# Moving value differences into the convolution stage, splitting the queries and keys of two heads at once, and running the value products four blocks behind the transposes with five buffers

## The chip, the cores and the metric

The kernel runs on one core of one Trainium2 chip. The metric is device microseconds of one execution, from the program's start to its end; lower is better. The time before is the median of three runs, 2573.38 us.

The core has five engines that each work through their own queue in order: TensorE (PE in the profile; PEld is its weight load), VectorE (DVE), ScalarE (ACT), GpSimd (POOL) and SyncE (SP), which here issues all DMA transfers. TensorE writes to PSUM, which this kernel deals out in tiles of 128 partitions by 512 float32 values (called banks here); the other work memory is SBUF. Scratch tensors lie in DRAM.

## The reference, cut to what matters

One layer of a decoder trunk over 1024 tokens of width 1024: token mixing, cross-attention, feed-forward. The token mixing has three branches that start from one input projection; the change concerns the first, stick-breaking attention with 16 heads of 64:

```python
for blk in range(seq // SB_BLOCK):
    z = jnp.einsum('bhtd,bhsd->bhts', qf[:, :, t0:t1], kf[:, :, :t1])
    causal = jnp.arange(t1)[None, :] < (t0 + jnp.arange(SB_BLOCK))[:, None]
    log_1mb = jnp.where(causal, jax.nn.log_sigmoid(-z), 0.0)
    tail = lax.cumsum(log_1mb, axis=3, reverse=True)
    w = jnp.where(causal, jnp.exp(z + tail), 0.0)
    outs.append(jnp.einsum('bhts,bhsd->bhtd', w, vf[:, :, :t1]))
```

The weight of key s for query t is the difference of two neighbouring running products of sigmoid(-z). So the sum over keys of weight times value can be written as a sum over keys of (running product minus 1) times the difference of two neighbouring values. The kernel does that: it needs the running products, from one scan, and the value differences v[s-1] - v[s].

## The kernel before, in words

Matrix products are exact to nearly float32 by splitting each operand into a high part (fp32r) and a low part (the remainder): a copy on ACT or POOL makes the high part (`hi_sb`, L96 or L92), a subtraction makes the low part (`lo_of`, L99), and three products replace one (`mm3`, L102 to L104; `acc3`, L220 to L222).

The stages of the program, by the trace of before: input norm and the token-major projections, which write the values to the scratch tensor `v_d` (shifted by one row, so that v[s-1] and v[s] are two loads of the same tensor); the convolution stage, 293 to 641 us; the attention stage, 641 to 1090 us; then the state-space mixer, the output projections, cross-attention and the feed-forward.

**Convolution stage** (L634 to L729). It makes 36 blocks of 128 output channels, two at a time in `pair` (L681): 12 pairs of convolution channels and 6 pairs of gate channels, mixed in the list `order` so that a gate pair stands after one or two convolution pairs and one gate pair stands last. A pair loads weights of 1 MB (L193), POOL makes sums of them (L196 to L199), ACT and DVE split them, and `winograd_pair` (L224) does seven products of 12 matmuls each and adds them up in two tiles `y` of the pool `t4`, which has six buffers named "b4" (shown as `b`). The first copies out of PSUM into `y` are L230, L232 and L234, the last one L688. Then `conv` (L663) runs four taps on ACT and DVE into another buffer (L665 to L669), or `gate` (L677) takes the sigmoid (L678) and stores to `g_d` (L679). Transposes of a convolution pair (`tail`, L651) run after the products of the next pair.

**Attention stage** (L736 to L937). The work is a list of 32 items m, two per head: the first half of the queries (four blocks of 128) and the second. A head pair is four items. For each item three lists are merged by position:

- `values` of item m: step i transposes key block i of the running products (L868) into PSUM, ACT makes the high part of the weights (L871, `wth`), DVE the low part (L872, `wtl`), and the two value products of block i - LAG follow (L880, L881), with LAG = 3. A first half has 4 key blocks and 7 steps, a second half 8 key blocks and 11 steps.
- `scores` of item m + 1: for each of four query blocks, products of q with the high and low key parts (L849, L850) into the pool `psc`, the sigmoid on ACT (L851) and the running product on DVE as one scan (L852). They take positions 0 to 0.7 of the item.
- a quarter of the projections of q and k for a later head pair (`dense`, L758 to L778, 24 to 27 matmuls of 512 columns), or at the end of late gate blocks. Their results are taken out of PSUM by `ev_q` (L786) and `ev_k` (L797): for each of the two heads a copy on ACT makes the high part on 64 partitions (L794, L806) and a subtraction on DVE the low part (L795, L807). For q the low part goes to the upper 64 partitions; for k SP copies high and low part to the upper 64 partitions (L808, L809), so that one product covers two of the terms.

The first block of a head also calls `differences` (L822): for an even head SP loads two 512 KB tiles from `v_d` (L828) and POOL subtracts them (L829); for each head POOL makes high and low part (L92, L99).

In this stage eight banks of PSUM are dealt out as 2 for the projections, 3 for scores (`psc`), 2 for transposes (`pst`) and 1 for value products. The weights' pool `wt` has four buffers for each part.

The order on each engine isn't written out by hand: a planner goes through the program in order of priority with a model of time, so a blocked instruction can be overtaken by a later one of the program, and the order that comes out is fixed in the program. What is fixed by hand are the lists merged above and a mark that keeps projection matmuls from going too far ahead (`issue_behind`, L773).

Of the kernel before, what the change touches and what calls it, by code (L numbers as in the profile page):

```python
# [8 lines left out]
F32 = mybir.dt.float32  # L9
# [3 lines left out]
ALU = mybir.AluOpType  # L13
# [22 lines left out]
def hybrid_block(ctx, tc, a, out, dbg=None):  # L36
# [20 lines left out]
    def scr(name, shape, dt=F32):  # L57
        return dram.tile(shape, dt, tag=name, name=name)
# [6 lines left out]
    bt_d = [scr(f"bt_d{g}", [S, P]) for g in range(NG)]  # L65

    v_d = scr("v_d", [S + 1, D])
    g_d = scr("g_d", [2 * D, S])
    o_d = scr("o_d", [D, S])

# [16 lines left out]
    def hi_sb(o, i, eng=None):  # L87
        if eng is None:
            turn[0] += 1
            eng = "pa"[turn[0] % 2]  # L90
        if eng == "p":
            G.tensor_scalar(o, i, 1.0, 0.0, ALU.mult, ALU.add)  # L92
        elif eng == "v":
            V.tensor_copy(o, i)
        else:
            A.activation(o, i, AF.Copy)  # L96
# [154 lines left out]
    with ExitStack() as pa:  # L251
# [382 lines left out]
        with ExitStack() as p1:  # L634
# [43 lines left out]
                A.activation(y, y, AF.Sigmoid)  # L678
                nc.sync.dma_start(g_d[f * P:(f + 1) * P, :], y)  # L679
# [12 lines left out]
            jobs = [(C_X + f * P, f, conv) for f in list(range(16, 24, 2)) + list(range(0, 16, 2))]  # L692
            gts = [(C_GA + f * P, f, gate) for f in range(0, 16 - LATE_GATES, 2)]
# [42 lines left out]
        with ExitStack() as p2:  # L736
# [45 lines left out]
            def qk_proj(hp):  # L782
                for j in range(2):
                    heads[2 * hp + j] = {}

                def ev_q(ps, half):  # L786
                    sl = slice(half * HALF, (half + 1) * HALF)
                    for j in range(2):
# [3 lines left out]
                        pj = ps[j * HD:(j + 1) * HD]  # L792
                        q = hd["q"]
                        A.activation(q[0:HD, sl], pj, AF.Copy)  # L794
                        V.tensor_tensor(q[HD:P, sl], pj, q[0:HD, sl].bitcast(F32), ALU.subtract)  # L795

                def ev_k(ps, half):  # L797
                    sl = slice(half * HALF, (half + 1) * HALF)
                    for j in range(2):
# [4 lines left out]
                        pj = ps[j * HD:(j + 1) * HD]  # L804
                        kh, kl = hd["kh"], hd["kl"]
                        A.activation(kh[0:HD, sl], pj, AF.Copy)  # L806
                        V.tensor_tensor(kl[0:HD, sl], pj, kh[0:HD, sl].bitcast(F32), ALU.subtract)  # L807
                        nc.sync.dma_start(kh[HD:P, sl].bitcast(F32), kh[0:HD, sl].bitcast(F32))  # L808
                        nc.sync.dma_start(kl[HD:P, sl].bitcast(F32), kl[0:HD, sl].bitcast(F32))  # L809

                return dense(C_Q + hp * P, ev_q), dense(C_K + hp * P, ev_k)

# [7 lines left out]
            dvs = {}  # L820

            def differences(h):  # L822

                j = h % 2
                if j == 0:
                    va, vb = [mk(vp, [P, NCH, P], F32, n, bufs=1) for n in ("va", "vb")]
                    for t, r in ((va, 0), (vb, 1)):
                        nc.sync.dma_start(t, v_d[r:S + r, h * HD:(h + 2) * HD].rearrange("(c p) d -> p c d", p=P))  # L828
                    G.tensor_tensor(va, va, vb, ALU.subtract)  # L829
                    dvs[0] = va  # L830
                dv = dvs[0][:, :, j * HD:(j + 1) * HD]
                vt = mk(vp, [P, NCH, P], F32R, "v")
                hi_sb(vt[:, :, 0:HD], dv, "p")
                lo_of(vt[:, :, HD:P], dv, vt[:, :, 0:HD], G)
                heads[h]["v"] = vt

            def scores(h, half, tb, ns_):
                def run():
                    hd = heads[h]
                    if half == 0 and tb == 0:  # L840
                        differences(h)
                    b = half * 4 + tb
                    L = (b + 1) * P
                    nt = mk(bp, [P, (half + 1) * HALF], F32, f"n{half}")
                    ns_.append(nt)
                    for s0 in range(0, L, HALF):
                        s1 = min(L, s0 + HALF)
                        ps = mk(psc, [P, HALF], F32, "sc")[:, :s1 - s0]
                        T.matmul(ps, hd["q"][:, b * P:(b + 1) * P], hd["kh"][:, s0:s1], start=True, stop=False)  # L849
                        marks.append(T.matmul(ps, hd["q"][:, b * P:(b + 1) * P], hd["kl"][:, s0:s1], start=False, stop=True))  # L850
                        A.activation(nt[:, s0:s1], ps, AF.Sigmoid, scale=-(HD ** -0.5))  # L851
                    V.tensor_tensor_scan(nt[:, 0:L][:, ::-1], nt[:, 0:L][:, ::-1], mask[:, S - L:][:, ::-1], 1.0, ALU.mult, ALU.max)  # L852
                return run

            ots = {}

            LAG = 3

            def values(h, half, ns_):

# [1018 lines left out]
```

## Time and profile before

| | us |
|---|---|
| median of 3 runs | 2573.38 |
| lowest and highest run | 2568.3, 2574.95 |
| the profiled execution, whole | 2569.1 |
| its span, first to last instruction | 2567.4 |
| convolution stage, from the trace | 293 to 641 |
| attention stage, from the trace | 641 to 1090 |

The profile is of one execution. For each group of instructions it gives the busy time, the mean duration of one in ns, and the idle time of the engine just before them with what ended that idle time (the releaser). In the lists of waits each line has the waiting engine and line, what it waited for, the total in us, the number of waits and the longest. In the windows view the busy time of each engine in a stretch is given with the number of instructions, then TensorE's granted clock as a share of the full one, the share of time that the DMA engines were busy, and what they moved in GB/s. In the timeline a line has the start, the duration, the instruction and, in brackets, the idle time before it. A matmul is drawn longer than the distance to the next one, since matmuls overlap in the array.

### The profile page before, as it was taken

Reading aid. Unit: us, or ns where it says so; the run is one execution under the profiler, and the core shown is the slowest. Engines: PE = TensorE matmul, PEld = TensorE weight load, DVE = VectorE, ACT = ScalarE, POOL = GpSimd, SP = SyncE. Lnnn points to the kernel's source line nnn. Section 1 sums busy time; section 2 is a strip of 40 time slices with the busy share of each in tenths; the row PEclk is TensorE's granted clock in tenths of the full one; section 3 lists DMA queues with packets and bytes.
Section 4 is the critical chain, followed back from the end, with each engine's and each line's share of the span. In section 5 each row is a group of like instructions: output and inputs, shape, how many; then the busy total and the mean of one; then the engine's idle time right before and its main releaser. Section 6 shows DMA issues by size and latency. Waiting matters only on the chain.

```text
span 2567.4 us, 32619 instructions
## 1 busy us (share of the span) xinstructions
PE 2485.3 (97%) x12026; PEld 2059.4 (80%) x12026; DVE 1817.7 (71%) x2143; ACT 1149.7 (45%) x2052; POOL 824.6 (32%) x666
## 2 busy tenths in 40 slices
PE   8999999999999999989999999999999999999998
PEld 6788788887788788777888788888787888887776
DVE  7685777767689898678788654415459666666997
ACT  6343455655466666556544302314233333334433
POOL 4331533221211121135655231100114333333675
PEclk9999999999999999989999999999999999999999
DMA  6441433333322222355332452321332232234322
GB/s 227 148 154 58 152 123 99 109 109 121 99 79 67 83 73 63 102 161 185 112 93 71 148 176 94 116 63 36 115 111 70 79 95 74 88 93 164 132 99 99
DMA packets 244331, 278.54 MB, mean 108 GB/s; under 512 B 15040, under 2 KB 171849, under 8 KB 243787
## 3 DMA queue, kind: packets, MB, share of 16 engines
q1 hardware_dynamic: 244170, 276.45, 34.0%
q8 instruction: 95, 1.56, 0.2%
q14 instruction: 66, 0.53, 0.1%
HBM read 197.87 MB, written 70.13 MB: 104 GB/s over the span
## 4 chain that ended last, share of the span: by engine, by line
PE 37%; DVE 7%; DMA 3%; issue 2%; POOL 1%; ACT 1%; SPq 0%; POOLq 0%; DVEq 0%; ACTq 0%
PE mm L222 5%; PE mm L220 5%; PE mm L221 5%; PE mm L102 4%; PE mm L104 3%; PE mm L103 3%; PE p L102 2%; PE p L103 2%; PE p L104 2%; DVE op L99 2%; PE pd L1090 1%; DMA gr<-gu_d 1%; DVE a L1755 1%; PE p L1468 1%; DMA wraw<-in_w_mix_out_dram 1%
## 5 line engine op out<-in xcount | busy, mean ns | idle before, releaser
L852 DVE TENSOR_TENSOR_SCAN n<-n,mask 128x128 f32<-128x128 f32 (+7 forms) x128 | 176.4, 1403 | 11.9 <-ACT n L851 9.2
L196 POOL TENSOR_TENSOR sf<-wr,wr 128x512 f32<-128x512 f32 x38 | 60.4, 1590 | 351.5 <-DMA wr<-in_w_gu_dram 129.3
L99 DVE TENSOR_TENSOR sw<-sf,sw 128x512 fp32r<-128x512 f32 x150 | 111.4, 754 | 58.9 <-ACT sw L96 58.4
L871 ACT ACTIVATE wth<-tr,mone 128x512 fp32r<-128x512 f32 x192 | 110.9, 580 | 73.3 <-PE tr L868 71.6
L96 ACT ACTIVATE sw<-sf 128x512 fp32r<-128x512 f32 x150 | 92.1, 626 | 106.8 <-PE mm L222 95.3
L872 DVE SCALAR_TENSOR_TENSOR wtl<-tr,wth 128x512 fp32r<-128x512 f32 x192 | 101.5, 546 | 40.0 <-ACT wth L871 38.5
L96 ACT ACTIVATE sw<-wr 128x512 fp32r<-128x512 f32 x113 | 70.8, 629 | 125.8 <-PE mm L222 124.2
L222 PE MATMUL mm<-h,sw 128*128 128x512 f32 x320 | 124.3, 389 | 1.8 <-DVE sw L99 1.8
L220 PE MATMUL mm<-h,sw 128*128 128x512 f32 x320 | 122.4, 391 | 3.1 <-ACT h L96 2.3
L221 PE MATMUL mm<-h,sw 128*128 128x512 f32 x320 | 124.5, 389 | 0.0
L102 PE MATMUL mm<-oth,bw 128*128 128x512 f32 (+1 forms) x320 | 122.0, 381 | 2.0 <-DVE a L1149 1.7
L104 PE MATMUL mm<-oth,bw 128*128 128x512 f32 (+1 forms) x320 | 119.1, 372 | 0.7 <-DVE bw L1136 0.5
L103 PE MATMUL mm<-otl,bw 128*128 128x512 f32 (+1 forms) x320 | 118.4, 370 | 0.0
L99 DVE TENSOR_TENSOR sw<-wr,sw 128x512 fp32r<-128x512 f32 x113 | 100.1, 889 | 16.1 <-ACT sw L96 16.1
L851 ACT ACTIVATE n<-sc 128x512 f32<-128x512 f32 (+1 forms) x192 | 89.1, 486 | 49.0 <-PE sc L850 25.0
L667 DVE SCALAR_TENSOR_TENSOR b<-b,prmT,b 128x1023 f32<-128x1023 f32 (+2 forms) x72 | 101.8, 1416 | 10.7 <-ACT b L665 10.2
L92 POOL TENSOR_SCALAR v<-va 128x512 fp32r<-128x512 f32 x16 | 20.0, 1255 | 273.7 <-PE av L881 147.9
L165 POOL TENSOR_SCALAR rstd<-ms 128x1 f32<-128x1 f32 x82 | 27.9, 341 | 244.6 <-ACT x L1370 103.5
L102 PE MATMUL p<-bw,h 128*128 128x512 f32 x256 | 98.9, 391 | 3.3 <-DVE x L1372 2.4
L104 PE MATMUL p<-bw,h 128*128 128x512 f32 x256 | 100.1, 392 | 0.0
L103 PE MATMUL p<-bw,h 128*128 128x512 f32 x256 | 99.8, 390 | 0.0
L198 POOL TENSOR_TENSOR sf<-wr 128x512 f32<-128x512 f32 x38 | 63.0, 1657 | 114.0 <-DVE sw L99 114.0
(592 smaller groups left out, 8141.5 us busy)
## 6 DMA issues: line engine op xcount, KB each, us to landing
wr<-in_w_gu_dram SPq DMA_DIRECT2D x80, 256.0 KB
wr<-in_w_in_dram SPq DMA_DIRECT2D x36, 512.0 KB
zr<-in_w_in_dram SPq DMA_DIRECT2D x32, 512.0 KB
gu_d<-t SPq DMA_DIRECT2D x44, 256.0 KB
wraw<-in_w_in_dram SPq DMA_DIRECT2D x20, 512.0 KB
xs_d<-b SPq DMA_DIRECT2D x32, 256.0 KB
s<-xs_d SPq DMA_DIRECT2D x32, 256.0 KB
s<-zs_d SPq DMA_DIRECT2D x32, 256.0 KB
```

The lines of the kernel that those rows point to most:

```text
L96: A.activation(o, i, AF.Copy)
L99: eng.tensor_tensor(o, i, hi.bitcast(F32), ALU.subtract)
L102: first = T.matmul(ps, sh, mh, start=start, stop=False)
L103: T.matmul(ps, sh, ml, start=False, stop=False)
L104: T.matmul(ps, sl, mh, start=False, stop=stop)
L220: T.matmul(ps, w[0][:, k, :], b[0][:, k, :], start=first and k == 0, stop=False, skip_group_check=True)
L221: T.matmul(ps, w[0][:, k, :], b[1][:, k, :], start=False, stop=False, skip_group_check=True)
L222: T.matmul(ps, w[1][:, k, :], b[0][:, k, :], start=False, stop=last and k == 3, skip_group_check=True)
L667: V.scalar_tensor_tensor(acc[:, sh:], y[:, :S - sh], cw(3 - sh, f), acc[:, sh:], ALU.mult, ALU.add)
L852: V.tensor_tensor_scan(nt[:, 0:L][:, ::-1], nt[:, 0:L][:, ::-1], mask[:, S - L:][:, ::-1], 1.0, ALU.mult, ALU.max)
L871: A.activation(wh[:, t0 * P:], pt[:, t0 * P:], AF.Identity, bias=mone)
L872: V.scalar_tensor_tensor(wl[:, t0 * P:], pt[:, t0 * P:], -1.0, wh[:, t0 * P:].bitcast(F32), ALU.add, ALU.subtract)
```

## The change

1. The value differences are made in the convolution stage. After a gate pair, `differences(hp)` loads the two tiles of a head pair into two "b4" buffers, DVE subtracts them, ACT and DVE split the differences of the two heads, and SP stores each head's result to a new scratch tensor `dv_d`. The first two gate pairs do this for two head pairs each, the other four for one. In the attention stage one load per head brings the split differences (`values_of`); POOL has no part in it any more.
2. For head pairs 1 to 7, q and k come out of PSUM for both heads in one copy and one subtraction on 128 partitions (`split`, into two tiles with one buffer each), and SP copies the parts of each head to their places: 4 copies per half for q, 8 for k, where before there were none for q and 4 for k. Head pair 0 is as before.
3. LAG goes from 3 to 4, the buffers of `wt` from 4 to 5, the banks for scores from 3 to 2 and those for transposes from 2 to 3.

```diff
+    dv_d = scr("dv_d", [S, NH * P])
...
+            def differences(hp):
+
+                va, vb = [mk(t4, [P, S], F32, "b4") for _ in range(2)]
+                for t, r in ((va, 0), (vb, 1)):
+                    nc.sync.dma_start(t.rearrange("p (c d) -> p c d", d=P),
+                                      v_d[r:S + r, hp * P:(hp + 1) * P].rearrange("(c p) d -> p c d", p=P))
+
+                def split():
+                    V.tensor_tensor(va, va, vb, ALU.subtract)
+                    dv = va.rearrange("p (c d) -> p c d", d=P)
+                    for j, t in enumerate((vb, va)):
+                        vt = t.bitcast(F32R).rearrange("p (c d) -> p c d", d=P)
+                        hi_sb(vt[:, :, 0:HD], dv[:, :, j * HD:(j + 1) * HD], "a")
+                        lo_of(vt[:, :, HD:P], dv[:, :, j * HD:(j + 1) * HD], vt[:, :, 0:HD])
+                        h = 2 * hp + j
+                        nc.sync.dma_start(dv_d[:, h * P:(h + 1) * P].rearrange("(c p) d -> p c d", p=P), vt.bitcast(F32))
+
+                return split
...
-            def pair(c0, f, fin, npool):
+            def pair(c0, f, fin, npool, beside=()):
...
+                for h in beside:
+                    differences(h)()
...
+            todo = NH // 2
             for i, j in enumerate(order):
                 if i == 8:
                     dt_columns()
-                pair(*j, 3 if i == 0 else 0)
+                n = 0 if j[2] is not gate else 2 if todo > 5 else 1
+                pair(*j, 3 if i == 0 else 0, range(NH // 2 - todo, NH // 2 - todo + n))
+                todo -= n
...
-            wt = pool(p2, "wt", 4, side="right")
+            wt = pool(p2, "wt", 5, side="right")
...
-            psc = pool(p2, "psc", 3, PSUM)
-            pst = pool(p2, "pst", 2, PSUM)
+            psc = pool(p2, "psc", 2, PSUM)
+            pst = pool(p2, "pst", 3, PSUM)
...
+                def split(ps):
+                    hi, lo = [mk(t2, [P, HALF], F32R, n, bufs=1) for n in ("hT", "lT")]
+                    A.activation(hi, ps, AF.Copy)
+                    V.tensor_tensor(lo, ps, hi.bitcast(F32), ALU.subtract)
+                    return hi.bitcast(F32), lo.bitcast(F32)
...
+                        if hp > 0:
+                            for r, t in enumerate(parts):
+                                nc.sync.dma_start(q[r * HD:(r + 1) * HD, sl].bitcast(F32), t[rows_])
+                        else:
...
+                        if hp > 0:
+                            for d, t in zip((kh, kl), parts):
+                                for r in range(2):
+                                    nc.sync.dma_start(d[r * HD:(r + 1) * HD, sl].bitcast(F32), t[rows_])
+                        else:
...
-            def differences(h):
-
-                j = h % 2
-                if j == 0:
-                    va, vb = [mk(vp, [P, NCH, P], F32, n, bufs=1) for n in ("va", "vb")]
-                    for t, r in ((va, 0), (vb, 1)):
-                        nc.sync.dma_start(t, v_d[r:S + r, h * HD:(h + 2) * HD].rearrange("(c p) d -> p c d", p=P))
-                    G.tensor_tensor(va, va, vb, ALU.subtract)
-                    dvs[0] = va
-                dv = dvs[0][:, :, j * HD:(j + 1) * HD]
-                vt = mk(vp, [P, NCH, P], F32R, "v")
-                hi_sb(vt[:, :, 0:HD], dv, "p")
-                lo_of(vt[:, :, HD:P], dv, vt[:, :, 0:HD], G)
-                heads[h]["v"] = vt
+            def values_of(h):
+
+                vt = heads[h]["v"] = mk(vp, [P, NCH, P], F32R, "v")
+                nc.sync.dma_start(vt.bitcast(F32), dv_d[:, h * P:(h + 1) * P].rearrange("(c p) d -> p c d", p=P))
...
-            LAG = 3
+            LAG = 4
```

More of the change, by code (lines that the diff above doesn't have):

```diff
@@ L784, in qk_proj @@
                     heads[2 * hp + j] = {}
+                def split(ps):
[3 more added lines that the diff above has]
+                    return hi.bitcast(F32), lo.bitcast(F32)
                 def ev_q(ps, half):
                     sl = slice(half * HALF, (half + 1) * HALF)
+                    if hp > 0:
+                        parts = split(ps)
                     for j in range(2):
@@ L803, in ev_k @@
                             hd["kl"] = mk(qk, [P, S], F32R, "kl")
-                        pj = ps[j * HD:(j + 1) * HD]
                         kh, kl = hd["kh"], hd["kl"]
[L806 to L809, printed above, removed]
+                        rows_ = slice(j * HD, (j + 1) * HD)
+                        if hp > 0:
+                            for d, t in zip((kh, kl), parts):
+                                for r in range(2):
+                                    nc.sync.dma_start(d[r * HD:(r + 1) * HD, sl].bitcast(F32), t[rows_])
+                        else:
+                            A.activation(kh[0:HD, sl], ps[rows_], AF.Copy)
+                            V.tensor_tensor(kl[0:HD, sl], ps[rows_], kh[0:HD, sl].bitcast(F32), ALU.subtract)
+                            for t in (kh, kl):
+                                nc.sync.dma_start(t[HD:P, sl].bitcast(F32), t[0:HD, sl].bitcast(F32))
                 return dense(C_Q + hp * P, ev_q), dense(C_K + hp * P, ev_k)
@@ L840, in run @@
                     if half == 0 and tb == 0:
-                        differences(h)
+                        values_of(h)
                     b = half * 4 + tb
```

9 lines of the change are left out of this document (5 added, 4 removed).

## The prediction

> **What bounds the kernel now.** I read the head of the page first, then the windows view cut at the stages that the change touches, then who waited for whom on the matmul engine there.
>
> ```profile
> span 2567.4 us, 32619 instructions
> ```
> ```profile
> PE 2485.3 (97%) x12026; PEld 2059.4 (80%) x12026; DVE 1817.7 (71%) x2143; ACT 1149.7 (45%) x2052; POOL 824.6 (32%) x666
> ```
> ```profile
> core 0: us, PE busy (x) PEld busy (x) DVE busy (x) ACT busy (x) POOL busy (x), PEclk, DMA share, GB/s
> 293.00:641.00 348.00, 344.33 (x1599) 285.68 (x1598) 256.41 (x269) 190.06 (x287) 102.96 (x63) 1.00 0.37 116
> 641.00:1090.00 449.00, 431.87 (x2311) 359.33 (x2310) 362.75 (x452) 261.40 (x508) 84.02 (x61) 1.00 0.29 80
> ```
> ```profile
> 700.00:1000.00 300.00, 290.01 (x1587) 242.43 (x1586) 265.39 (x325) 188.39 (x366) 57.13 (x36) 1.00 0.26 73
> ```
>
> PE bounds the program: 97% busy, at the full granted clock in these stages. Only PE's idle time can be won. The convolution stage (293 to 641 us) leaves it 348 − 344.33 = 3.7 us, the attention stage (641 to 1090 us) 449 − 431.87 = 17.1 us. The last row is the even middle of attention: 300 − 290.01 = 10.0 us of PE idle, with DVE busy 265.39 of 300, 88%. What ends PE's idle time, first in the attention stage, then in the convolution stage:
>
> ```profile
> PE av L881 <- DVE wtl L872: 10.5, 15, 1.2
> PE pst L102 <- ACT state L1060: 2.8, 1, 2.8
> PE mm L102 <- DVE qs L795: 1.4, 1, 1.4
> PE tr L868 <- DVE wtl L872: 1.2, 2, 1.0
> ```
> ```profile
> PE mm L220 <- ACT b L230: 2.7, 1, 2.7
> ```
>
> Columns: total us, times, longest. 11.7 us of attention's 17.1 us are PE waiting for DVE's low half of the transposed weights (L872), nearly all at the value products (av). The second row is the start of the state-space stage, behind the change. The single row below is the convolution stage's largest wait. The timeline shows how one such wait comes about; PE, then DVE:
>
> ```profile
> 798.92 0.39 PE L849 MATMUL sc<-kh,qs 128*128 128x512 f32 x1
> 799.15 0.39 PE L850 MATMUL sc<-kl,qs 128*128 128x512 f32 x1
> ...
> 799.83 0.28 PE L850 MATMUL sc<-kl,qs 128*128 128x256 f32 x1
> 801.34 0.39 PE L881 MATMUL av<-wtl,v 128*128 128x256 f32 x1 [1.23 <-DVE wtl L872]
> ...
> 826.17 0.33 PE L880 MATMUL av<-wth,v 128*128 128x256 f32 x1
> 826.72 0.39 PE L881 MATMUL av<-wtl,v 128*128 128x256 f32 x1 [0.22 <-DVE wtl L872]
> ```
> ```profile
> 797.17 3.66 DVE L852 TENSOR_TENSOR_SCAN n<-n,mask 128x768 f32<-128x768 f32 x2
> 800.86 0.62 DVE L872 SCALAR_TENSOR_TENSOR wtl<-tr,wth 128x256 fp32r<-128x256 f32 x2
> ```
>
> 512-column matmuls start 0.23 us apart (798.92, 799.15), though each is drawn 0.39 us long. DVE ran two scans for 3.66 us, the low half came only at 800.86, and PE, in order, stood still. The second wait, at 826.72, has a drawn idle of 0.22 us, but start to start is 0.55 us where a 256-column product needs half of 0.23, so it costs about 0.4 us. Fifteen such waits over eight head pairs are about two per pair: one long, one short.
>
> **The change part by part.**
>
> *Queries and keys split at once (head pairs 1 to 7).* Per pair and 512-column half, two heads each for q and k took 4 ACT copies and 4 DVE subtractions on 64 partitions.
>
> ```profile
> L795 DVE TENSOR_TENSOR qs<-mm,qs 64x512 fp32r<-64x512 f32 x32 | 22.1, 689 | 3.9 <-ACT qs L794 2.7
> ```
> ```profile
> L806 ACT ACTIVATE kh<-mm 64x512 fp32r<-64x512 f32 x32 | 19.0, 593 | 21.1 <-PE mm L104 18.5 <-DVE kl L807 2.2
> ```
> ```profile
> L872 DVE SCALAR_TENSOR_TENSOR wtl<-tr,wth 128x512 fp32r<-128x512 f32 x96 | 65.1, 680 | 36.1 <-ACT wth L871 35.5
> ```
>
> 680 ns for 128 partitions against 689 for 64: partitions cost nothing, so half of the instructions go. Seven pairs × 4 × 0.689 = 19.3 us of DVE and 28 × 0.593 = 16.6 us of ACT leave a stage of about 430 us. In their place SP issues 24 copies per pair instead of 8. At 0.46 us each
>
> ```profile
> L808 SPq DMA_DIRECT2D kh<-kh x32: 461/462/583, 656.4 to 1009.8; - x32
> ```
>
> that is 11 us of SP in the some 50 us of a pair (801.34 to 851.01 is one period of the pattern, and 6 periods fill 700 to 1000). Behind them in SP's queue stand weight and value loads and the stores of finished heads; the first use of a key half is a quantum (a quarter of a pair, 12 us) later. The split halves have one buffer each, so ACT's next split, a quantum later, waits until these copies have landed, and behind it on ACT stand the sigmoids and high halves that PE waits for. I cost both at nothing; the price without that cover is rival three.
>
> *Differences leave attention.* POOL loses five operations per head pair. They slowed DVE:
>
> ```profile
> L852 DVE TENSOR_TENSOR_SCAN n<-n,mask 128x384 f32<-128x384 f32 x16 | 15.0, 938 | 1.7 <-ACT n L851 1.7
> ```
> ```profile
> L852 DVE TENSOR_TENSOR_SCAN n<-n,mask 128x256 f32<-128x256 f32 x16 | 11.3, 708 | 0.2
> L852 DVE TENSOR_TENSOR_SCAN n<-n,mask 128x128 f32<-128x128 f32 x16 | 11.2, 700 | 0.0
> ```
>
> 128 columns less save 938 − 708 = 230 ns once and then nothing; at 230 the shortest scan should take 0.48 us, and 16 × 0.22 = 3.5 us of DVE come back (the first score block of a head, whose scan has 128 columns, is what starts POOL's differences, so they run side by side). DVE's attention load falls from 362.75 to about 362.75 − 19.3 − 3.5 = 340 us, 6% less. SP no longer waits for POOL before its v_d loads; one load of 512 KB per head takes the place of two per head pair. None of this is PE time by itself: it makes the waits shorter.
>
> *Values four behind, five weight buffers, three transpose banks, two score banks.* Between low half and product lies one more step. A half-0 item has 4 + 3 steps now and 4 + 4 then, so in 12 us a step is 1.5 us, and the long wait was 1.23 us. With DVE also 6% freer I take four fifths of 11.7 us as gone, 9.4 us, and of the part that the idle column does not show (some 8 × 0.4 us) 3 us: 12.4 us. Bounds: 17 us, all of the stage's idle, to 0, if another wait takes the place. What is late next is the score bank (rival two). The start of the state-space stage (2.8 us) could shift either way as DVE or SP comes free sooner or later; I take 0, and 3 us to both sides.
>
> *Differences in the convolution stage.* Each head pair adds two loads and two stores of 512 KB, a subtraction, two copies and two low halves.
>
> ```profile
> L669 DVE TENSOR_TENSOR b<-b,b 128x1024 f32<-128x1024 f32 x24 | 34.1, 1420 | 13.1 <-ACT b L668 13.1
> ```
> ```profile
> L99 DVE TENSOR_TENSOR sw<-wr,sw 128x512 fp32r<-128x512 f32 x49 | 46.0, 943 | 15.2 <-ACT sw L96 15.2
> ```
> ```profile
> L96 ACT ACTIVATE sw<-wr 128x512 fp32r<-128x512 f32 x48 | 30.0, 629 | 18.6 <-PE mm L222 18.5
> ```
> ```profile
> L678 ACT ACTIVATE b<-b 128x1024 f32<-128x1024 f32 x12 | 12.7, 1059 | 4.0 <-DVE b L241 3.9
> ```
> ```profile
> L196 POOL TENSOR_TENSOR sf<-wr,wr 128x512 f32<-128x512 f32 x38 | 60.4, 1590 | 351.5 <-DMA wr<-in_w_gu_dram 129.3
> ```
>
> DVE: 8 × (1.42 + 2 × 0.943) = 26.4 us, 256.41 to 283 of 348, 81%. ACT: 16 × 0.629 = 10 us, to 200. Both stay under PE, and the ACT row of weights (sw) shows it waiting for PE (18.5 us) to free weight buffers, so weights are ahead of their products. The loads and stores add 16 MB to a stage at 116 GB/s (40 MB), at a DMA share of 0.37: room again. By the Trainium skill (SBUF — State Buffer, "Who interferes with whom") a DVE operation with two SBUF inputs and a GpSimd operation reading SBUF exclude one another for a whole instruction; that speaks against moving this work beside POOL's sums of weights, and by it the 30% of the 24 new DVE operations that meet a POOL sum (102.96 of 348 us) would each wait half of its 1.59 us, an estimated 6 us more on DVE. The trace agrees in kind, and its 943 ns hold such waits already, against 680 for the low half out of PSUM (L872). What PE would feel is late buffers (the v_d loads wait in SP's queue for a work buffer, and the next weights' loads stand behind them), and its floor here has no slack: I take +2.5 us (one more wait like L230's 2.7), between −2 (that one gone) and the rival's 28.
>
> **Sum.** −12.4 + 2.5 = −10 us: 2567.4 to about 2557 in span. The profiled execution took 2569.1 us in all, 1.7 over its span and 4.3 under the median 2573.38 of the runs; against that median the forecast is 2563.4.
>
> **The rivals.**
>
> One, slower: the convolution stage's six work buffers ("b4"). A gate pair holds two, the convolution pair before it two until its transposes, each difference two more from load to landed store.
>
> ```profile
> 641.22 0.33 SPq L679 DMA_DIRECT2D g_d<-b  x1
> 641.64 0.39 SPq L828 DMA_DIRECT2D va<-v_d  x1
> ```
> ```profile
> L829 POOL TENSOR_TENSOR va<-va,vb x8: 2386/3270/3392, 648.0 to 986.4; 128x1024 f32<-128x1024 f32 x8
> ```
> ```profile
> L751 DVE MEMSET mask<- x1: 485/485/485, 644.8 to 644.8; 128x512 uint32 x1
> ```
> ```profile
> L232 ACT ACTIVATE b<-mm 128x512 f32<-128x512 f32 x17 | 10.2, 602 | 2.1 <-DMA g_d<-b 2.1
> ```
>
> A load takes 648.0 − 641.64 = 6.4 us, a store at least 644.8 − 641.22 = 3.6 us (the mask waits for that memory), so a difference holds its buffers 6.4 + 1.4 + 2 × (0.63 + 0.94) + 3.6 = 14.5 us. PE can run ahead of the next pair's first copy out of PSUM by two products, 24 × 0.23 = 5.5 us. If that copy must wait for the gate's own buffer (addition and copies, two sigmoids of 1.06 us, store: about 8 us after the pair), PE loses 2.5 us; where a second difference is ahead of it in line for that buffer, 14.5 − 5.5 = 9 us. Two gate pairs have two differences and four have one: 2 × 9 + 4 × 2.5 = 28 us, 2563.4 + 28 = 2591. It decides where such a copy starts over 5.5 us into a pair. For it: L232 waits 2.1 us for a store already. Against: only one such wait in 17. 14%.
>
> Two, no change: two score banks. ACT stands still before the sigmoid until transposes free its target,
>
> ```profile
> ACT n L851 <- PE tr L868: 23.1, 24, 2.4
> ```
>
> 24 times, 1 us each. A third bank hid that from PE; if half shows, 11.5 us come back: 2575. Against: PE waits for ACT nowhere in its list here. 12%.
>
> Three, no change: copies late.
>
> ```profile
> SPq L808 <- ACT n L851: 61.5, 16, 14.3
> ```
>
> SP waited 61.5/16 = 3.8 us behind a sigmoid before a key copy, 14.3 at worst. Eight issues take 3.7 us and landing at most the load's 6.4, 10.1 of 12 us; 3.8 us more overruns by 1.9, and seven pairs, once each, lose 13 us: 2576. By the Trainium skill (DMA: Bandwidth & Descriptors, "Anatomy of one DMA") a transfer has a fixed cost of about 2 us; with it the estimate is 3.7 + 2.3 and the margin 6 us, and this rival would fall; no row here shows the landing of such a copy. 6%.
>
> Four, it does not do what it says: DVE still runs the scans first and the low half comes just as late relative to its product; only 2 or 3 us go, 0 net: 2573. 5%.
>
> Five, more: nearly all 17 us of idle go and the convolution stage costs nothing: 2556. 6%.
>
> **How the numbers follow.** A measurement of this kernel tells about 0.3%, 7.7 us, from nothing, so faster is below 2565.7 and slower above 2581.1. The forecast has 57%; by its bounds 2557 to 2570, about 50 of these are faster and 7 the same. With five: 56% faster. Rival one is slower from some 18 of its 28 us on, 12 slower and 2 same; two 10 same and 2 slower; three 4 same and 2 slower; four same: 28% same, 16% slower. The range 2553 to 2581 holds the forecast, five, four, nearly all of two and three, and the little of one that ends as the same: some 84%. The forecast's own range is 2557 to 2570.
>
> **What would show it.** Right: L881's wait for L872 under 3 us; DVE's share in the middle of attention near 82%; L852 at 128 columns under 0.5 us; convolution stage within 3 us of 348. Wrong: PE waiting for sigmoids at L849 (two), for kh, kl or qs copies (three), for L230 or L232 behind dv_d stores (one), or the pattern at L881 unchanged (four).

## The result, and the profile after

The changed kernel takes 2555.27 us, median of 6 runs (2552.04 to 2558.16); the kernel before takes 2573.63 us, median of 6 runs beside them. The ratio is 0.993, 95% interval 0.9919 to 0.9941: 18.4 us less. The profiled execution took 2553.45 us, its span is 2551.7 us against 2567.4.

The windows view of the changed kernel, first over the two stages at the cuts used for before, then over the even middle of attention (columns as before):

```profile
293.00:641.00 348.00, 343.62 (x1589) 283.90 (x1588) 277.33 (x290) 196.35 (x298) 104.09 (x63) 1.00 0.52 158
641.00:1090.00 449.00, 436.65 (x2348) 365.14 (x2347) 343.60 (x436) 253.83 (x498) 32.22 (x27) 0.99 0.46 124
```
```profile
700.00:1000.00 300.00, 297.29 (x1633) 249.79 (x1632) 245.65 (x309) 174.71 (x349) 14.74 (x7) 1.00 0.47 121
```

In the middle of attention DVE went from 265.39 to 245.65 us, POOL from 57.13 to 14.74. PE's idle time fell from 10.0 to 2.7 us, and the better measure is the count beside it: 1633 matmuls in 300 us where there were 1587 (a count takes large and small products alike, so it is a rough measure too). In the convolution stage DVE went from 256.41 to 277.33 us and the stage did 10 matmuls less by 641 us, so it is late by some 2 us.

The waits of PE in the changed kernel, attention and the start of the state-space stage, then the convolution stage:

```profile
PE dec L1070 <- DMA colrows<-sum_d: 5.7, 1, 5.7
PE tr L900 <- DVE wtl L904: 3.1, 13, 0.4
PE pst L105 <- DVE bl L100: 1.7, 1, 1.7
PE pst L103 <- DVE state L1095: 0.4, 1, 0.4
```
```profile
PE mm L221 <- ACT b L231: 2.9, 2, 2.4
PE tr L658 <- DVE b L670: 0.7, 2, 0.4
PE mm L221 <- ACT b L708: 0.7, 1, 0.7
```

Lines have moved by 1 to 32: transposes are L900, high and low halves L903 and L904, value products L912 and L913, the first score product L881. The wait of the value products for the low half (10.5 us) is gone from the list. In its place stand 13 short waits of the transposes themselves for the low half, that is for a transpose bank, 3.1 us in all. The first, third and fourth rows belong to the start of the state-space stage, which the window now takes in because attention ends earlier; the wait of 5.7 us is in the trace of before too, with 6.4 us (L1038), and so is no effect of the change.

Where the 15.7 us of span went can be read from three places. The rows of the first score product and of the last value product give the first and last start (after "min/median/max"); before, then after:

```profile
L849 PE MATMUL sc<-kh,qs x192: 218/389/506, 661.1 to 1060.7; 128*128 128x512 f32 x96, 128*128 128x128 f32 x32, 128*128 128x256 f32 x32, 128*128 128x384 f32 x32
```
```profile
L881 PE MATMUL av<-wtl,v x192: 220/419/486, 680.0 to 1084.7; 128*128 128x512 f32 x96, 128*128 128x384 f32 x32, 128*128 128x256 f32 x32, 128*128 128x128 f32 x32
```
```profile
L881 PE MATMUL sc<-kh,qs x192: 218/389/476, 663.1 to 1057.2; 128*128 128x512 f32 x96, 128*128 128x128 f32 x32, 128*128 128x256 f32 x32, 128*128 128x384 f32 x32
```
```profile
L913 PE MATMUL av<-wtl,v x192: 222/377/481, 677.9 to 1071.5; 128*128 128x512 f32 x96, 128*128 128x384 f32 x32, 128*128 128x256 f32 x32, 128*128 128x128 f32 x32
```

Up to the first score product: 661.1 to 663.1, 2.0 us later. Most of this is the differences in the convolution stage: over all traces of the study this start lies at 661.1 to 662.3 us without them and at 661.9 to 664.4 us with them, and two traces of one program (e7 and e8 below) differ by 1.5 us in it. From there to the last value product, called the attention length below: 1084.7 − 661.1 = 423.6 to 1071.5 − 663.1 = 408.4, 15.2 us shorter. From there to the end of the span: 1482.7 to 1480.2, 2.5 us shorter. The sum is −15.7.

### The profile page after: what moved, and what is told of

Its sections match the earlier page's. It is cut to its first block, busy times and chain, and to the rows that moved or that the text cites. A ratio compares the mean times of both kernels' runs of the same rounds, so it can differ in the third digit from the quotient of the medians.

```text
span 2551.7 us, 32774 instructions
## 1 busy us (share of the span) xinstructions
PE 2477.9 (97%) x12026; PEld 2059.0 (81%) x12026; DVE 1808.6 (71%) x2139; ACT 1139.9 (45%) x2040; POOL 768.7 (30%) x626
## 5 line engine op out<-in xcount | busy, mean ns | idle before, releaser
L884 DVE TENSOR_TENSOR_SCAN n<-n,mask 128x128 f32<-128x128 f32 (+7 forms) x128 | 171.0, 1351 | 39.2 <-ACT n L883 38.7
L93 POOL TENSOR_SCALAR whi<-wraw 128x1024 fp32r<-128x1024 f32 x10 | 18.7, 1868 | 396.8 <-PE mm L104 329.2
L904 DVE SCALAR_TENSOR_TENSOR wtl<-tr,wth 128x512 fp32r<-128x512 f32 x192 | 99.7, 546 | 33.4 <-ACT wth L903 33.1
L903 ACT ACTIVATE wth<-tr,mone 128x512 fp32r<-128x512 f32 x192 | 106.6, 582 | 24.9 <-PE tr L900 22.6
L100 DVE TENSOR_TENSOR sw<-wr,sw 128x512 fp32r<-128x512 f32 x113 | 94.9, 843 | 19.0 <-ACT sw L97 19.0
L900 PE MATMUL tr<-ident,n 128*128 128x128 f32 x576 | 98.2, 275 | 3.1 <-DVE wtl L904 3.1
L100 DVE TENSOR_TENSOR zl<-zr,zh 128x512 fp32r<-128x512 f32 x84 | 75.6, 913 | 34.5 <-ACT zh L97 34.3
```

The source lines that it names most:

```text
L100: eng.tensor_tensor(o, i, hi.bitcast(F32), ALU.subtract)
L903: A.activation(wh[:, t0 * P:], pt[:, t0 * P:], AF.Identity, bias=mone)
L904: V.scalar_tensor_tensor(wl[:, t0 * P:], pt[:, t0 * P:], -1.0, wh[:, t0 * P:].bitcast(F32), ALU.add, ALU.subtract)
```

## The experiments

Three parts of the change can be put in and left out: the **differences** (in the convolution stage), the **split** (of two heads at once), and the third part, which is again three things: the **banks** (2 for scores and 3 for transposes instead of 3 and 2), **LAG** 4 instead of 3, and the fifth weight buffer. The theory at the start was that of the prediction, called L: products one step later find their low half ready, and the banks are there to allow it. The rival, theory D in the expectations, was that DVE simply has less to do. Theory B, from the fourth run on, is that the third transpose bank does it alone.

| run | differences | split | banks | LAG | weight buffers | us | ratio to before, 95% interval | attention length |
|---|---|---|---|---|---|---|---|---|
| before | | | 3+2 | 3 | 4 | 2573.63 | 1 | 423.6 |
| e1 | yes | | 3+2 | 3 | 4 | 2570.74 | 0.9996 (0.9986 to 1.0006) | 421.6 |
| e2 | yes | yes | 3+2 | 3 | 4 | 2567.70 | 0.9982 (0.9972 to 0.9991) | 418.4 |
| e4 | yes | yes | 3+2 | 4 | 5 | 2572.34 | 1.0005 (0.9995 to 1.0015) | 427.5 |
| e6 | | | 2+3 | 3 | 4 | 2558.86 | 0.9941 (0.9925 to 0.9956) | 409.9 |
| e9 | | | 2+3 | 4 | 4 | 2558.40 | 0.9949 (0.9937 to 0.9961) | 414.5 |
| e10 | yes | | 2+3 | 3 | 4 | 2558.13 | 0.9943 (0.9931 to 0.9955) | 410.1 |
| e3 | yes | | 2+3 | 4 | 5 | 2560.46 | 0.9960 (0.9945 to 0.9975) | 411.5 |
| e12 | yes | yes | 2+3 | 2 | 4 | 2552.12 | 0.9919 (0.9906 to 0.9931) | 407.6 |
| e5 | yes | yes | 2+3 | 3 | 4 | 2549.58 | 0.9907 (0.9891 to 0.9923) | 405.8 |
| e8 | yes | yes | 2+3 | 4 | 4 | 2554.78 | 0.9927 (0.9913 to 0.9941) | 408.3 |
| e7 | yes | yes | 2+3 | 4 | 4 | 2553.77 | 0.9927 (0.9912 to 0.9942) | 408.3 |
| after | yes | yes | 2+3 | 4 | 5 | 2555.27 | 0.9930 (0.9919 to 0.9941) | 408.4 |
| e11 | yes | yes | 2+2 | 3 | 4 | 2567.34 | 0.9980 (0.9971 to 0.9990) | 418.8 |

Each ratio is to runs of the kernel before on the same chip. The attention length comes from each run's trace, as above, before rounding; it is of one execution, and the two traces of one program (e7, e8) agree on it.

**e1: the differences alone.** The kernel before with the change's `differences(hp)`, its calls from `pair`, and `values_of(h)`; pools, LAG, `ev_q` and `ev_k` stay. The places where it meets the kernel before:

```diff
-            def differences(h):
+            def values_of(h):
...
+                vt = heads[h]["v"] = mk(vp, [P, NCH, P], F32R, "v")
+                nc.sync.dma_start(vt.bitcast(F32), dv_d[:, h * P:(h + 1) * P].rearrange("(c p) d -> p c d", p=P))
...
-                        differences(h)
+                        values_of(h)
```

> The kernel before with the first part of the change alone (value differences made in the convolution stage; queries and keys split per head, LAG 3, 4 weight buffers, 3 score and 2 transpose banks as before). Theory L (the waits at the value products go because products run one step later): the waits L881 on L872 stay near 10 us, the convolution stage costs 2 us, the time is 2572 to 2576. Theory D (they go because DVE has less to do): POOL's conflict with the scans is gone, 3.5 us of DVE's 363, so a fifth of the waits goes: about 2572. Theory F (POOL out of attention is itself the gain, by SP no longer waiting for POOL): 2562 or less.

No change in time: 0.9996. POOL leaving attention shortens it by 2.0 us and the convolution stage gives that back (first score product at 663.9, 2.8 us later). The waits at the value products stayed:

```profile
PE av L894 <- DVE wtl L885: 9.7, 13, 1.2
```

**e2: the change without its third part.**

```diff
-            wt = pool(p2, "wt", 5, side="right")
+            wt = pool(p2, "wt", 4, side="right")
...
-            psc = pool(p2, "psc", 2, PSUM)
-            pst = pool(p2, "pst", 3, PSUM)
+            psc = pool(p2, "psc", 3, PSUM)
+            pst = pool(p2, "pst", 2, PSUM)
...
-            LAG = 4
+            LAG = 3
```

> The changed kernel with its third part undone (LAG 3, 4 weight buffers, 3 score and 2 transpose banks); differences in the convolution stage and the split of two heads at once stay. Theory L: the waits at the value products return with some 8 to 10 us, the time is 2568 to 2573. Theory D: DVE has 20 us less to do in attention, so most waits stay away: 2556 to 2561.

2567.7, just under theory L's 2568 to 2573 and far from theory D's 2556 to 2561. With DVE as free as in the changed kernel (242.04 of 300 us in the middle) PE still waits 6.5 us at the value products, and 3.2 us at another place (L912 waits for L921, which empties the one bank of the value products), so a freer DVE is not what took the waits away:

```profile
PE av L913 <- DVE wtl L904: 6.5, 9, 1.2
PE av L912 <- DVE oT L921: 3.2, 6, 0.5
```
```profile
700.00:1000.00 300.00, 292.24 (x1598) 246.11 (x1597) 242.04 (x302) 170.94 (x344) 6.28 (x6) 1.00 0.45 117
```

**e3: the change without the split of two heads.** `ev_q` and `ev_k` as in the kernel before; of the latter:

```diff
-                    if hp > 0:
-                        parts = split(ps)
...
+                        pj = ps[j * HD:(j + 1) * HD]
...
+                        A.activation(kh[0:HD, sl], pj, AF.Copy)
+                        V.tensor_tensor(kl[0:HD, sl], pj, kh[0:HD, sl].bitcast(F32), ALU.subtract)
+                        nc.sync.dma_start(kh[HD:P, sl].bitcast(F32), kh[0:HD, sl].bitcast(F32))
+                        nc.sync.dma_start(kl[HD:P, sl].bitcast(F32), kl[0:HD, sl].bitcast(F32))
```

> The changed kernel with its second part undone (queries and keys of every head pair taken out of PSUM per head, 8 copies and 8 subtractions per pair); differences in the convolution stage, LAG 4, 5 weight buffers, 2 score and 3 transpose banks stay. Theory L: nearly all of the gain stays, 2555 to 2559. Theory D: DVE is as loaded as before, most of the gain goes: 2566 to 2572.

2560.46: most of the gain stays, 11.2 us of it beside its own runs of before, as theory L had it, with 1.5 us more than its range. The split shortens attention by 411.5 − 408.4 = 3.1 us here.

**e4: the change with the old banks.**

```diff
-            psc = pool(p2, "psc", 2, PSUM)
-            pst = pool(p2, "pst", 3, PSUM)
+            psc = pool(p2, "psc", 3, PSUM)
+            pst = pool(p2, "pst", 2, PSUM)
```

> The changed kernel with 3 score banks and 2 transpose banks as before; LAG 4 and 5 weight buffers stay. If the third transpose bank is what lets transposes run ahead (theory L needs both): PE waits for a transpose bank (L900 on L904) and the time is 2560 to 2566. If the longer distance alone does it: 2554 to 2558. If the second score bank cost something (rival two of the prediction), this kernel is faster than the changed one: below 2552.

All of the gain is gone: 1.0005. This is outside every expectation. LAG 4 and five buffers with two transpose banks make attention longer than LAG 3 does (427.5 against 418.4 in e2), and the waits at the value products stand as before, though the product now runs four steps behind:

```profile
PE av L913 <- DVE wtl L904: 9.3, 14, 1.1
PE av L912 <- DVE oT L921: 3.2, 6, 0.5
PE tr L900 <- DVE wtl L904: 1.3, 2, 1.0
```

That broke theory L in its stated form. What was left was the banks, so the next experiments took them alone.

**e5: the change with LAG 3 and four buffers, the new banks kept.**

```diff
-            wt = pool(p2, "wt", 5, side="right")
+            wt = pool(p2, "wt", 4, side="right")
...
-            LAG = 4
+            LAG = 3
```

> The changed kernel with LAG 3 and 4 weight buffers, but 2 score and 3 transpose banks as in the change. Theory B (the third transpose bank alone takes the waits away, the distance is nothing): 2554 to 2558, no wait of L912 or L913 on L904. Theory L (both are needed): the waits at the value products are back with 5 to 10 us, 2562 to 2568.

2549.58: the lowest median of the study, 4.4 us under the range of theory B, and no wait of the value products for the low half is left in its list, as theory B had it. It is 5.7 us under the changed kernel by the medians (the two intervals overlap, 0.9923 and 0.9919, and they ran beside different runs of before). The closer comparison is with the kernel that has LAG 4 and the same four buffers (e7 and e8 below, beside the same runs of before): all four runs of e5, 2548.87 to 2550.50, lie under all twelve of that kernel, 2551.32 to 2557.73. In the middle of attention PE has no drawn idle time left, and does 1671 matmuls where before did 1587:

```profile
700.00:1000.00 300.00, 300.00 (x1671) 256.27 (x1670) 251.08 (x314) 178.97 (x356) 13.71 (x7) 1.00 0.49 125
```

**e6: the kernel before with the new banks and nothing else.** Two lines:

```diff
-            psc = pool(p2, "psc", 3, PSUM)
-            pst = pool(p2, "pst", 2, PSUM)
+            psc = pool(p2, "psc", 2, PSUM)
+            pst = pool(p2, "pst", 3, PSUM)
```

> The kernel before with only its banks changed (2 for scores, 3 for transposes); differences on POOL in attention, queries and keys split per head, LAG 3, 4 weight buffers. Theory B: 12 to 14 us of attention go without any cost in the convolution stage, 2558 to 2562. Theory L: 2567 to 2572. Theory D (room on DVE is needed as well): the banks alone give half, 2564 to 2567.

2558.86, a ratio of 0.9941: 13.8 us under the 2572.70 of its own runs of before, three quarters of the change's gain from two numbers. POOL still makes the differences in attention (58.44 us in the middle) and DVE is as busy as before (269.22 of 300 us); neither had to change for this gain. Who waited for whom on ACT points at what the bank does. Before, and then e6, from 641 to 1085 us:

```profile
ACT wth L871 <- PE tr L868: 71.6, 72, 3.5
ACT n L851 <- PE sc L850: 25.0, 36, 2.9
ACT n L851 <- PE tr L868: 23.1, 24, 2.4
```
```profile
ACT n L851 <- PE sc L850: 54.8, 55, 3.7
ACT wth L871 <- PE tr L868: 43.8, 76, 2.5
...
ACT n L851 <- PE tr L868: 1.7, 1, 1.7
```

With two banks ACT stood still 71.6 us before a high half because the transposes had not been done, and 23.1 us before a sigmoid because the tile that it writes was still to be transposed. With three banks these are 43.8 and 1.7 us. ACT now waits for scores instead (54.8); of what follows from a late sigmoid, PE's own list in e6 has only 1.3 us (transposes that wait for a scan).

The timing of the key blocks shows it directly. Each trace has 192 of them; taking the rows of L868, L872 and L881 (or their later numbers) in order of time, one can follow each block, and the averages below are over the 144 blocks of the twelve middle heads:

| | before | e2 | e4 | e6 | e9 |
|---|---|---|---|---|---|
| transpose banks, LAG | 2, 3 | 2, 3 | 2, 4 | 3, 3 | 3, 4 |
| first transpose of a block to its product with the low half, us | 4.36 | 4.37 | 4.47 | 6.08 | 6.22 |
| end of its low half to that product, us | 1.28 | 1.64 | 1.83 | 2.33 | 2.57 |
| of all 192 products, those that start within 0.1 us of the end of their low half | 21 | 15 | 23 | 1 | 1 |

With a third bank the transposes run further ahead of the products, and the low half is ready in time. LAG does next to nothing to this distance: 4.37 to 4.47 us with two banks (e2 to e4, with the fifth buffer), 6.08 to 6.22 us with three (e6 to e9).

**e7 and e8: the changed kernel with four weight buffers.** The kernel of e7 is the same as that of e8. The expectation of e7 was written for another kernel (the one of e9), so it does not apply; e7 is a second measurement of e8.

```diff
-            wt = pool(p2, "wt", 5, side="right")
+            wt = pool(p2, "wt", 4, side="right")
```

> The kernel before with 2 score banks, 3 transpose banks and LAG 4, but 4 weight buffers, since a fifth does not fit beside the tiles of the differences. Theory B: as the kernel with the banks alone, 2558 to 2562. Theory L: with 4 buffers the transposes wait for a weight buffer (fewer steps ahead), 2562 to 2567; if the fifth buffer is not needed, 2558 to 2561.

> The changed kernel with 4 weight buffers in place of 5, all else as in the change. If the fifth buffer is what the freed memory buys: PE or ACT waits for weight buffers and the time is 2560 to 2566. If three banks of transposes hold what is ahead anyway: 2554 to 2557.

2553.77 (e7) and 2554.78 (e8), both at 0.9927 where the changed kernel has 0.9930: the fifth buffer does nothing. The pair also shows what two runs of one program differ by, 1.0 us in the median, and 2.8 us in the profiled spans (2550.0 and 2552.8).

**e9: the kernel before with the new banks and LAG 4.** As e6, and:

```diff
-            LAG = 3
+            LAG = 4
```

> The kernel before with 2 score banks, 3 transpose banks and LAG 4, 4 weight buffers; nothing else of the change. Theory B (the third transpose bank takes the waits away, and LAG 4 beside it only adds short waits at the transposes, 3 us in the changed kernel): some 5 us slower than the kernel before with the banks alone, 2562 to 2566. Theory L (the distance adds to the banks): 2552 to 2557.

2558.40, no different from e6 in time, and between what the two theories had. In the attention stage it goes the way of theory B: attention is 414.5 − 409.9 = 4.6 us longer than in e6, and the part behind it is 4.3 us shorter (span less last value product: 1479.3 against 1483.6), though nothing was changed there. TensorE's mean granted clock may be most of this: it was 0.991 in the profiled execution of e6 and 0.993 in that of e9, and 0.002 of 2556 us is by an estimate up to 5 us. The middle of attention does 1606 matmuls, against 1650 in e6:

```profile
700.00:1000.00 300.00, 293.43 (x1606) 245.96 (x1604) 262.14 (x330) 188.82 (x371) 54.04 (x39) 1.00 0.27 73
```
```profile
700.00:1000.00 300.00, 298.38 (x1650) 251.68 (x1649) 269.22 (x336) 192.14 (x377) 58.44 (x39) 1.00 0.28 75
```

**e10: differences and banks, without the split.** As e3, and:

```diff
-            wt = pool(p2, "wt", 5, side="right")
+            wt = pool(p2, "wt", 4, side="right")
...
-            LAG = 4
+            LAG = 3
```

> Differences in the convolution stage and the banks (2 for scores, 3 for transposes); queries and keys split per head, LAG 3, 4 weight buffers. If the split of two heads at once is worth several us once the banks are there (DVE freer): 2557 to 2561, as the kernel before with the banks alone plus the convolution stage's 2 us. If it is worth nothing: 2548 to 2552.

2558.13, as expected if the split counts: e5, which has it, is 8.6 us faster, and the two intervals do not meet. Half of that is in attention (410.1 to 405.8); the other half is behind it (1482.8 to 1477.4 us from the last value product to the end of the span), in code that is the same, and is not explained.

**e11: two banks for scores and two for transposes.** As e5, and:

```diff
-            pst = pool(p2, "pst", 3, PSUM)
+            pst = pool(p2, "pst", 2, PSUM)
```

> The changed kernel with LAG 3, 4 weight buffers, 2 score banks and only 2 transpose banks (seven banks in use in attention). Theory B: the third transpose bank is what counts, so the waits at the value products are back and the time is that of the kernel without the third part, 2566 to 2571. If fewer score banks were the gain, by the order that they give: 2549 to 2556.

2567.34, the time of e2 (2567.70). So with two transpose banks, two score banks are as good as three, and the gain is that of the third transpose bank: from e11 to e5, which differ by it alone, attention is 418.8 − 405.8 = 13.0 us shorter. The waits have moved, though: 0.3 us at L913, 6.1 us at L912, and the rest in gaps too short to be drawn; the count of matmuls in the middle is the one to trust, 1590 (1598 in e2):

```profile
PE av L912 <- DVE oT L921: 6.1, 7, 0.9
...
PE tr L900 <- DVE wtl L904: 2.4, 7, 0.4
```
```profile
700.00:1000.00 300.00, 291.30 (x1590) 244.65 (x1589) 242.47 (x301) 176.65 (x343) 11.73 (x6) 1.00 0.45 116
```

**e12: LAG 2.** The edit to the changed kernel:

```diff
-            wt = pool(p2, "wt", 5, side="right")
+            wt = pool(p2, "wt", 4, side="right")
...
-            LAG = 4
+            LAG = 2
```

> The changed kernel with LAG 2 and 4 weight buffers, 2 score and 3 transpose banks. Theory B with a limit (a distance under the number of transpose banks leaves no room between low half and product): the waits at the value products return, 2556 to 2566. If the distance is nothing at all: 2548 to 2552, as with LAG 3.

2552.12, just above the range for "the distance is nothing", with 1.8 us of waits at L913 back:

```profile
PE av L913 <- DVE wtl L904: 1.8, 4, 0.6
```

Attention is 407.6 us, 405.8 with LAG 3, 408.3 with LAG 4 (four buffers): here LAG moves it by 2.5 us at most. Without the differences and the split it moves it by 4.6 us (e6 to e9). By the times, LAG 2 and LAG 3 can't be told apart: the runs of e12 go from 2548.13 to 2554.36.

## Why the prediction was right, and where its reason was not

The forecast was 10 us less; measured were 18.4 us in the medians and 15.7 us in the profiled spans. The stated range, 2553 to 2581, holds the 2555.27; the forecast's own range, 2557 to 2570, misses it by 1.7 us. That the time came out near the forecast is in good part luck: most of it was priced for a step that gave nothing, and a number of the same change that had no price gave it instead. Point by point:

- **What bounds the kernel** was right. PE was the bound, its waits for the low half in attention were what could be won, and in the changed kernel they are gone.
- **Attention, −12.4 us**: measured −15.2. The price came from the right waits, for the wrong cause (next point); the part in gaps that are not drawn was larger than the 3 us set for it. The bound by idle time (17 us with everything) was a little low: in e5 attention is 423.6 − 405.8 = 17.8 us shorter, since PE has idle time that no idle column shows.
- **The step that failed** is the one that says what removes the waits: "Between low half and product lies one more step", with "DVE also 6% freer". The prediction took that step as 1.5 us of distance. Measured, the pause between the end of a low half and its product grew by 0.24 us with LAG (e6 to e9), while the third transpose bank made it longer by 1.05 us (before to e6). LAG 4 lengthened attention in each pair of kernels that differ by it: 409.9 to 414.5 (e6, e9) and 405.8 to 408.3 (e5, e8) by LAG alone; 418.4 to 427.5 (e2, e4) and 410.1 to 411.5 (e10, e3) by LAG and the fifth buffer, which does nothing by e8. Why it does so was not settled. The differences and the split together, which leave DVE freer, gave 5.2 us of attention (before to e2). The third transpose bank gave 13.7 us (before to e6), 12.6 us (e2 to e5) and 19.1 us (e4 to after), each time taken from the scores, and 13.0 us by itself (e11 to e5). I listed the bank in the heading of that paragraph and gave it no price. How it acts is shown by the table under e6; that the third bank is the cause is shown by e4, e6 and e11. The signs that the prediction set for being right all came true (no wait of the value products for the low half, DVE at 82% in the middle, the short scan under 0.5 us, the convolution stage within 3 us), and none of them could tell LAG from the bank.
- **Queries and keys**: half of the instructions did leave (28 subtractions over 128 partitions took 678 ns each, in the row below; 689 had been the price of 64 partitions), and the split took 3.2, 4.3 and 3.1 us off attention (e1 to e2, e10 to e5, e3 to after). Under "None of this is PE time by itself" I had put it at nothing of its own, only as help for the waits at the value products. The row is from the groups of the changed kernel, DVE, 641 to 1085 us:

```profile
L814 DVE TENSOR_TENSOR lT<-mm,hT 128x512 fp32r<-128x512 f32 x28 | 19.0, 678 | 2.8 <-ACT hT L813 2.8
```

- **Differences in the convolution stage, +2.5 us**: measured +2.0 in the changed kernel, where two traces of one program (e7, e8) differ by 1.5 us. DVE's work there went up by 277.33 − 256.41 = 21 us against 26 forecast, and the 6 us more that were estimated for meeting POOL's sums did not show. The scans got as much faster as expected: the 128-column one took 415 ns instead of 700 (the row below). In all, moving the differences is worth nothing in time (e1, and e6 against e10).

```profile
L884 DVE TENSOR_TENSOR_SCAN n<-n,mask 128x128 f32<-128x128 f32 x16 | 6.6, 415 | 1.5 <-ACT n L883 1.3
```

- **Behind the stage, 0 and 3 us to both sides**: measured −2.5. In the other runs the part behind attention lies between 1475.8 (e12) and 1487.4 us (e11), without any change to its code. This scatter is as large as LAG's or the split's effect on the total. Part of it may be TensorE's granted clock, which differs from one execution to the next: from 1070 to 1220 us, right behind attention, it was 0.90 in the trace of e11 and 0.93 in that of e12, and over the whole execution 0.990 and 0.995. These two traces are also extremes of their kernels: e11's is of a run of 2572.51 us where its median is 2567.34, e12's is of its fastest run. The clock doesn't explain all: e5, with 0.992, has 1477.4 us there, and e10, with 0.993, 1482.8. The planner's order and the state in which the stage starts differ from kernel to kernel too; what they add was not settled.
- **From spans to medians**: the profiled execution of before was 4.5 us under its median and that of after 1.8 us; the remaining 2.7 us between −15.7 and −18.4 are that.

The rivals: *one* (work buffers) happened once. One first copy waited for a store of differences, 5.7 us on ACT, and cost PE next to nothing (2.9 us at L231 after, 2.7 us at L230 before):

```profile
L231 ACT ACTIVATE b<-mm 128x512 f32<-128x512 f32 x17 | 10.0, 588 | 8.0 <-DMA dv_d<-b 5.7 <-DVE b L670 2.3
```

*Two* (score banks) had the sign wrong: the sigmoid's waits for transposes, the row it was built on, were themselves an effect of too few transpose banks, and fell from 23.1 to 1.7 us in e6. *Three* (copies late): no wait of PE for a query or key part is in the list of the changed kernel. *Four* (the pattern at the value products unchanged) did not happen, but it describes e4, LAG 4 with the old banks: 9.3 us of waits there and 2572.34 us. *Five* had the nearest number, 2556: it said that nearly all of attention's idle time goes and that the convolution stage costs nothing. In the middle of attention 7.3 of 10.0 us went, and the convolution stage cost some 2 us.

## What to carry to other kernels

When an in-order engine waits for the last link of a chain, look at which link starts late before moving the consumer back: here ACT's waits for transposes (71.6 us) pointed to a chain that began late for want of a PSUM bank, and a consumer one step later only made the stage longer, by 1.4 to 9.1 us. A change with several numbers in it is worth running one number at a time: the two bank numbers alone gave 13.8 us where the whole change gave 18.4, the differences gave nothing, and the change with LAG 3 and four weight buffers has a lower median still, 2549.58 us. Compare stages by the work done in a fixed window, not by the idle time drawn: two score and two transpose banks (e11 against e2) took the waits at L913 from 6.5 to 0.3 us and no time away. A sign that would come true under a rival's cause as well doesn't test the cause.

## What the runs showed of the hardware that was not expected

A busy share of PE near 100% still hides a per cent or so: in the same 300 us PE was drawn busy for 300.00 us with 1671 matmuls (e5) and for 297.29 us with 1633 (after), 0.9% more busy time and 2.3% more matmuls. Even at 300.00 us the count differs: 1662 in e10 and 1659 in e12. A matmul's drawn length hides gaps, since a product of 512 columns is drawn 0.39 us long where the next can start 0.23 us after it.

The time of one program went with TensorE's mean granted clock in some kernels and not in others. Of e11's twelve runs the one at 0.995 took 2564.71 us and the two at 0.990 took 2572.51 and 2572.67; of e1's eleven runs the one at 0.990 took 2569.78 us, and two at 0.993 took 2568.52 and 2573.43.
